# Top-k masks, the order of the search, and the order of weight halves in a hybrid attention block

## The chip, the cores and the metric

The kernel runs on one core of a Trainium2 chip. A core has a matrix engine (TensorE, PE), three engines for elementwise work (VectorE or DVE, ScalarE or ACT, GpSimd or POOL), a queue that issues transfers (SyncE or SP) and 16 DMA engines. Each engine takes its instructions in a fixed order and waits on semaphores for the others. The metric is the device time of one execution in microseconds (us).

## The reference

One decoder block on x of 1024 tokens by 1024 channels, in float32. Two branches read the same projection `h @ w_in`: RWKV-7 time mixing, and sparse attention in which an indexer picks 256 keys for each query. The two are gated, projected and added to x; a squared-ReLU MLP follows. What matters here is the selection:

```python
logits = jnp.einsum('bqhd,bsd->bqhs', qi_b, ki)
score = jnp.einsum('bqh,bqhs->bqs', wi_b, jax.nn.relu(logits)).astype(f32)
causal = key_pos[None, :] <= qpos[:, None]
score = jnp.where(causal[None], score, -jnp.inf)
_, idx = lax.top_k(score, topk)                 # topk = 256
...
s = jnp.einsum('bqhd,bqkd->bqhk', q_b, k_sel) * (ATT_HEAD_DIM ** -0.5)
s = jnp.where(valid[:, :, None, :], s, -jnp.inf)
p = jax.nn.softmax(s, axis=-1)
```

Of equal scores at the threshold, `top_k` takes those with the lowest index.

## The kernel before

Work goes through in phases: norm and transposition of x; the projections of the attention branch; indexer scores; the search for each query's 256th largest score; masks; attention; the RWKV recurrence; gates and output projection; the MLP. Matrix products keep float32 accuracy by splitting both operands into a high and a low part and adding three products (`mm3`, L242 to L245, and `mm3y`, L195 on, which goes through `mm`, L190). A weight tile is loaded (`st`), its high part is taken by ScalarE (L210) and its low part by GpSimd, or by VectorE where that is asked for (L211). Split weights live in a ring of three buffers (`w`).

*Projections by tokens* (`in_a`, L293 on). For the keys and values, the indexer queries and the attention queries, 256 columns at a time. The weights come as two tiles, `ws[0]` for the input channels 0 to 511 and `ws[1]` for 512 to 1023. For each half of the tokens and each pair of 128-token tiles, one accumulation buffer (`dn`, two of them) takes tile j = 0 through all eight channel blocks k, then tile j = 1. ScalarE evicts it (L306), and rotary embedding follows on GpSimd (L381) and VectorE (L382 to L386).

*Gate projections* (`gates`, L444 on). A generator of 16 units of eight steps for one half of the tokens, 24 matmuls to a unit, then an eviction by ScalarE (L453) and a transfer out (L454). It fills PE while the scores are made; what is left runs after the last query projection.

*Selection* (`select`, L538 on). Query blocks 0 and 1 have no more than 256 keys and need no search. The six others are searched by two generators: `([3, 4, 5], True)` counts with ScalarE, `([2, 6, 7], False)` with VectorE. A score is turned into a sortable 32-bit key, whose high and low 16 bits are searched one after the other, 16 bisection steps each. ScalarE counts by summing signs (L593) with the bookkeeping on GpSimd (L595 to L603); VectorE counts with a comparison that accumulates (L578) and does its own bookkeeping (L583, L584). Between the two searches the low keys are clipped against the high result (L614 to L616, on VectorE for both generators). After the second, the threshold is put together from both results (L621 to L626) and the mask of each block is made on VectorE (L634 to L641): 0 for a chosen key, -BIG for another, written over the scores `sc[b]`.

*Order.* The two generators are advanced in turns (loop at L825). In turns 19 and later, the list `SPREAD` says how many steps of the RWKV projections (`rwkv_in`, eight steps to a half of one unit, 24 matmuls and an eviction) are pulled after the turn. `RIN[0]`, 114, is the number of those steps ahead of attention; `RIN[0] - QF - early` of them, with `early` what the turns have taken, come after the masks, then the load and split of the first queries (`q_split`), then `QF` = 8 more. The eviction of such a half is ScalarE's at L673 and VectorE's at L674 (and, for the column between halves, L679 and L681). A planner lays out each engine's queue from this program order with a simulated time; `in_order` and `after` add order without a wait: an operation passed to `in_order` stands in VectorE's queue behind the one last stored in `own["V"]`. During the searches the first count of each step and each eviction at L674 are chained in this way.

*Buffers.* The mask's three work tiles (`ge`, `eq`, `cs`), the keys, ScalarE's junk output and attention's scores and split queries share one ring of six buffers (`t4`). Attention (`att_s`, L765 on) adds `sc[b]` to the raw scores and takes the maximum in one operation (L782).

## Time and profile before

| | |
|---|---|
| median of 3 runs | 1784.76 us (1780.63 to 1793.0) |
| the profiled execution | 1787.29 us |
| its span, first to last instruction | 1785.5 us |
| PE busy over the span | 1685.5 us (94%) |
| VectorE busy over the span | 1336.4 us (75%) |
| mean granted clock of PE | 0.972 |

The durations below are of the one profiled execution. In a row of the profile, "L593 ACT ACTIVATE jk<-room,neg" is line 593, ScalarE, an activation that writes the tile `jk` from `room` and `neg`. A group gives count, busy time and mean; a wait gives who waited, for whom, the total in us, how often, and the longest. "PEld" is the loading of weights into PE, beside the matmuls. A row of the order of time starts with start and duration in us, and may end with the idle time before it and what ended it.

### The profile page before, as it was taken

How to read it: one execution, taken by the hardware profiler on the slowest of the kernel's cores; microseconds unless marked ns; L12 is line 12 of the kernel's file. 1: busy time of each engine (PE TensorE's matmuls, PEld its weight loads, DVE VectorE, ACT ScalarE, POOL GpSimd, SP SyncE). 2: the span in 40 equal slices, each digit the busy share in tenths (PEclk: the TensorE clock that was granted, in tenths of full speed). 3: DMA queues.
4: the chain of work that ended last, by engine and by line, in shares of the span. 5: the costliest groups of instructions: out<-in, count | busy, mean ns of one | idle time of the engine just before them, and what ended most of it. 6: DMA issues, size and time to landing. Idle time of an engine off the chain costs nothing.

```text
span 1785.5 us, 27137 instructions
## 1 busy us (share of the span) xinstructions
PE 1685.5 (94%) x9554; PEld 1415.8 (79%) x9554; DVE 1336.4 (75%) x2610; ACT 894.3 (50%) x1751; POOL 821.8 (46%) x749
## 2 busy tenths in 40 slices
PE   6999899889999989998999998999999999999997
PEld 6988887778888777786777887877888888888885
DVE  6689989986777374767665546799988875865988
ACT  5376667547777434354535425553444444444443
POOL 1522564334443243344424532486766655545552
PEclk9999999999999998999887999999999999999999
DMA  5230254223211455355345567416444358643544
GB/s 176 78 118 27 81 154 118 73 69 112 100 30 52 138 148 139 91 146 164 102 116 166 172 196 282 124 54 212 154 157 168 130 185 307 204 147 101 146 144 142
DMA packets 268287, 242.04 MB, mean 136 GB/s; under 512 B 64284, under 2 KB 206934, under 8 KB 268150
## 3 DMA queue, kind: packets, MB, share of 16 engines
q1 hardware_dynamic: 268150, 240.30, 43.1%
q8 instruction: 75, 1.23, 0.3%
q14 instruction: 62, 0.51, 0.1%
HBM read 164.76 MB, written 75.50 MB: 135 GB/s over the span
## 4 chain that ended last, share of the span: by engine, by line
PE 56%; DVE 21%; DMA 7%; ACT 5%; issue 5%; POOL 4%; SPq 1%; POOLq 0%; DVEq 0%; ACTq 0%
PE up L190 24%; PE dn L190 11%; PE sm L190 9%; DVE jk L578 2%; PE sm L193 2%; PE ch L190 2%; DVE w L1348 2%; DMA zt<-zd 2%; PE acc L190 2%; PE dn L245 1%; PE dn L244 1%; PE dn L243 1%; ACT jk L593 1%; DVE LT L958 1%; DVE Z L1020 1%
## 5 line engine op out<-in xcount | busy, mean ns | idle before, releaser
L190 PE MATMUL dn<-hT,w 128*128 128x512 f32 (+1 forms) x1488 | 380.0, 403 | 11.4 <-ACT ev L453 4.5
L190 PEld LDWEIGHTS dn<-hT,w 128*128 128x128 f32 (+1 forms) x1488 | 274.1, 189 | 72.0 <-ACT ev L453 5.3
L190 PE MATMUL up<-h,w 128*128 128x512 f32 x1344 | 310.4, 391 | 6.1 <-DVE w L1348 3.3
L190 PEld LDWEIGHTS up<-h,w 128*128 128x128 f32 x1344 | 251.1, 188 | 62.4 <-DVE w L1348 5.0
L1348 DVE TENSOR_TENSOR w<-st,w 128x512 fp32r<-128x512 f32 x216 | 215.5, 1031 | 75.6 <-ACT w L1347 75.5
L211 POOL TENSOR_TENSOR w<-st,w 128x1024 fp32r<-128x1024 f32 (+2 forms) x75 | 183.3, 2445 | 186.8 <-ACT w L210 153.1
L190 PE MATMUL up<-w 128*128 128x512 f32 x1008 | 246.1, 390 | 3.6 <-DVE w L1348 3.5
L190 PEld LDWEIGHTS up<-w 128*128 128x128 f32 x1008 | 188.7, 188 | 45.4 <-DVE w L1348 6.4
L1347 ACT ACTIVATE w<-st 128x512 fp32r<-128x512 f32 x216 | 128.1, 625 | 159.2 <-PE up L190 50.9
L1641 POOL TENSOR_TENSOR st<-wb,wb 128x512 f32<-128x512 f32 x80 | 120.0, 1503 | 94.5 <-DVE w L1348 74.3
L1503 POOL TENSOR_TENSOR c<-st 128x512 f32<-128x512 f32 x80 | 125.4, 1576 | 50.2 <-DMA st<-in_w_ffn_up 23.7
L210 ACT ACTIVATE w<-st 128x1024 fp32r<-128x1024 f32 (+2 forms) x91 | 94.6, 1041 | 46.6 <-PE acc L245 15.4
L1514 POOL TENSOR_TENSOR C<-C 128x512 f32<-128x512 f32 x64 | 75.9, 1186 | 56.5 <-ACT C L1513 56.5
L578 DVE TENSOR_SCALAR_CACHE_REDUCE jk<-room,cand 128x384 bf16<-128x384 int16 (+2 forms) x96 | 97.1, 1012 | 2.9
L593 ACT ACTIVATE jk<-room,neg 128x512 bf16<-128x512 int16 (+2 forms) x96 | 78.5, 819 | 34.4 <-POOL neg L601 26.7
L243 PE MATMUL dn<-w,hT 128*128 128x256 f32 (+1 forms) x320 | 92.4, 291 | 3.5 <-ACT w L210 2.6
L244 PE MATMUL dn<-w,hT 128*128 128x256 f32 (+1 forms) x320 | 92.1, 289 | 3.5 <-DVE w L211 3.5
L788 POOL TENSOR_SCALAR sm<-sm,rs 128x128 f32<-128x128 f32 (+7 forms) x64 | 47.7, 747 | 102.5 <-DVE rs L787 58.6
L245 PE MATMUL dn<-w,hT 128*128 128x256 f32 (+1 forms) x320 | 91.8, 289 | 0.0
L1348 DVE TENSOR_TENSOR w<-c,w 128x512 fp32r<-128x512 f32 x80 | 82.9, 1048 | 0.4 <-ACT w L1347 0.3
L190 PE MATMUL sm<-w 128*128 128x512 f32 x288 | 81.0, 389 | 0.0
L1347 ACT ACTIVATE w<-c 128x512 fp32r<-128x512 f32 x80 | 48.8, 626 | 58.3 <-PE up L190 46.0
(332 smaller groups left out, 3519.9 us busy)
## 6 DMA issues: line engine op xcount, KB each, us to landing
st<-hcd SPq DMA_DIRECT2D x112, 256.0 KB
st<-in_w_in SPq DMA_DIRECT2D x54, 512.0 KB
st<-in_w_ffn_up SPq DMA_DIRECT2D x36, 512.0 KB
hcd<-C SPq DMA_DIRECT2D x16, 1024.0 KB
wb<-in_w_ffn_down SPq DMA_DIRECT2D x64, 256.0 KB
hcd<-kc SPq DMA_DIRECT2D x16, 768.0 KB
zd<-ev SPq DMA_DIRECT2D x20, 512.0 KB
gzd<-ev SPq DMA_DIRECT2D x32, 256.0 KB
```

The costliest lines, as they stand in the source:

```text
L190: pe(nc.tensor.matmul(*args, **kw))
L210: nc.scalar.activation(hi, st[0:rows, 0:n], AF.Copy)
L211: (eng or nc.gpsimd).tensor_tensor(lo, st[0:rows, 0:n], hi.bitcast(F32), op=OP.subtract)
L243: nc.tensor.matmul(ps, l[0], r[0], start=start, stop=False, skip_group_check=shared)
L244: nc.tensor.matmul(ps, l[0], r[1], start=False, stop=False, skip_group_check=shared)
L245: nc.tensor.matmul(ps, l[1], r[0], start=False, stop=stop, skip_group_check=shared)
L578: ins = nc.vector.tensor_scalar(jk[:, 0:(b + 1) * P], src[b], cand[:, j:j + 1], None, op0=OP.is_ge, op1=OP.add, accum_out=cnt[:, j:j + 1])
L593: nc.scalar.activation(junk, src[b], AF.Sign, bias=neg[:, j:j + 1], accum_out=cnt[:, j:j + 1])
L1347: nc.scalar.activation(hi, src, AF.Copy)
L1348: return eng.tensor_tensor(lo, src, hi.bitcast(F32), op=OP.subtract)
L1503: nc.gpsimd.tensor_tensor(c, src, blocks[LEFT[p][2]], op=OP.add if LEFT[p][1] == "+" else OP.subtract)
L1641: nc.gpsimd.tensor_tensor(c, src, wblocks[RIGHT[p][2], f], op=OP.add if RIGHT[p][1] == "+" else OP.subtract)
```

## The change

Five things are edited.

- `select`, masks: the comparison that counts is now "not above the threshold" and its result `ge` is kept; equality is written as 0 or BIG, so that its running sum counts in BIG; the number of equal keys still wanted comes from the count alone, `(count + 256 - n) * BIG`; and the last operation puts `ge * -BIG` and the chosen equal keys together. BIG becomes a power of two. Six operations over a block's columns become five.
- `select`, order: ScalarE's generator yields three more turns before its thresholds and masks, and each generator yields after each mask but its last. A mask's first operation is in order behind `own["V"]`, its last is stored there. So VectorE's own blocks 2, 6, 7 come first, then 3, 4, 5.
- `SPREAD` has five entries more, 8 steps each, so that an RWKV half with its eviction is pulled behind each of the first five masks; 40 steps fewer come after the masks.
- `gates` keeps its evictions in a list, and the first Sign of ScalarE's low search is put behind the third last of the 16 of `gates(1, ...)` in ScalarE's queue.
- `in_a`: the weight half `kh` becomes the outermost loop inside an accumulation buffer: both tiles take channel blocks 0 to 3, then both take 4 to 7.

```diff
--- before.py
+++ after.py
@@ -32,9 +32,9 @@
 FF = 4096
 DEC = float(np.exp(-0.5))
 NEG = -3.0e38
-BIG = 1.0e30
+BIG = float(2 ** 100)
 PE_WINDOW = 32
-SPREAD = [0, 0, 0, 0, 0, 8, 8, 8, 8, 0, 8, 8, 8, 0, 8]
+SPREAD = [0, 0, 0, 0, 0, 8, 8, 8, 8, 0, 8, 8, 8, 0, 8, 8, 8, 8, 8, 8]
 FILL = [8, 2, 40, 3, 6, 22]
 AHEAD = [6, 6, 6, 0, 0, 0, 0, 0, 1, 1, 0, 10]
 FIN_LAG = 5
@@ -297,12 +297,11 @@
             z = ev4()
             for pr in range(2):
                 ps = dense()
-                for j in range(2):
+                for kh, j, k in [(kh, j, 4 * kh + i) for kh in range(2) for j in range(2) for i in range(4)]:
                     t = 2 * pr + j
-                    for k in range(8):
-                        mm3(ps[:, j * 256:j * 256 + n], [hT[half][k][:, s_, t * P:(t + 1) * P] for s_ in range(2)],
-                            [ws[k // 4][:, s_, k % 4, :] for s_ in range(2)],
-                            start=(k == 0 and j == 0), stop=(k == 7), shared=True)
+                    mm3(ps[:, j * 256:j * 256 + n], [hT[half][k][:, s_, t * P:(t + 1) * P] for s_ in range(2)],
+                        [ws[kh][:, s_, k % 4, :] for s_ in range(2)],
+                        start=(k == 0 and j == 0), stop=(k == 7), shared=True)
                 nc.scalar.activation(z[:, pr * 512:(pr + 1) * 512].rearrange("p (t c) -> p t c", t=2)[:, :, 0:n],
                                      ps.rearrange("p (t c) -> p t c", t=2)[:, :, 0:n], AF.Copy)
             evac(half, z)
@@ -441,6 +440,8 @@
         return [(w_in[:, C_GATE + u * P:C_GATE + (u + 1) * P].rearrange("(k p) n -> p k n", p=P), [8, P])
                 for u in range(16)]
 
+    gate_ev = []
+
     def gates(hf, mul, ws):
         for u in range(16):
             w = next(ws)
@@ -450,7 +451,7 @@
                     mul(ps, w[:, a_, k, :], hT[hf][k][:, b_, :], start=(k == 0 and i == 0), stop=(k == 7 and i == 2))
                 if k == 7:
                     e = ev4()
-                    nc.scalar.activation(e[:, 0:512], ps, AF.Copy)
+                    gate_ev.append(nc.scalar.activation(e[:, 0:512], ps, AF.Copy))
                     nc.sync.dma_start(gz_dram[u // 8, u % 8, :, hf * 512:(hf + 1) * 512], e[:, 0:512])
                 yield
 
@@ -590,7 +591,10 @@
             for k in range(15, -1, -1):
                 for j, b in enumerate(blocks):
                     junk = t4b("jk", (b + 1) * P, BF16)
-                    nc.scalar.activation(junk, src[b], AF.Sign, bias=neg[:, j:j + 1], accum_out=cnt[:, j:j + 1])
+                    ins = nc.scalar.activation(junk, src[b], AF.Sign, bias=neg[:, j:j + 1],
+                                               accum_out=cnt[:, j:j + 1])
+                    if src is lo and k == 15 and j == 0:
+                        after(gate_ev[-3], ins)
                 up, _ = step_of(k)
                 nc.gpsimd.tensor_tensor(ok, cnt, need, op=OP.add)
                 nc.gpsimd.tensor_scalar(ok, ok, 1.0, -1.0, op0=OP.min, op1=OP.max)
@@ -618,9 +622,11 @@
             yield
         yield from search(lo)
         thr, ti = sm_("thr"), sm_("ti", I32)
+        for _ in range(3 if act else 0):
+            yield
         in_order(nc.vector.tensor_copy(ti, th))
         nc.vector.tensor_scalar(ti, ti, 16, None, op0=OP.logical_shift_left)
-        nc.vector.tensor_scalar(tl, cand, 32768.0, None, op0=OP.add)
+        in_order(nc.vector.tensor_scalar(tl, cand, 32768.0, None, op0=OP.add))
         nc.vector.tensor_tensor(ti, ti, tl, op=OP.bitwise_or)
         nc.vector.tensor_scalar(tl, ti, 31, 0x7FFFFFFF, op0=OP.arith_shift_right, op1=OP.bitwise_and)
         nc.vector.tensor_tensor(thr.bitcast(I32), ti, tl, op=OP.bitwise_xor)
@@ -631,14 +637,16 @@
             ge = t4("ge")[:, 0:n]
             eq = t4("eq")[:, 0:n]
             cs = t4("cs")[:, 0:n]
-            nc.vector.tensor_scalar(ge, sc[b], t_ap, None, op0=OP.is_ge, op1=OP.add, accum_out=cnt[:, j:j + 1])
-            nc.vector.tensor_scalar(eq, sc[b], t_ap, None, op0=OP.is_equal)
+
+            in_order(nc.vector.tensor_scalar(ge, sc[b], t_ap, None, op0=OP.is_le, op1=OP.add,
+                                             accum_out=cnt[:, j:j + 1]))
+            nc.vector.tensor_scalar(eq, sc[b], t_ap, BIG, op0=OP.is_equal, op1=OP.mult)
             nc.vector.tensor_tensor_scan(cs, eq, eq, 0.0, op0=OP.add, op1=OP.max)
-            nc.vector.scalar_tensor_tensor(gen[:, j:j + 1], cs[:, n - 1:n], float(TOPK), cnt[:, j:j + 1],
-                                           op0=OP.add, op1=OP.subtract)
+            nc.vector.tensor_scalar(gen[:, j:j + 1], cnt[:, j:j + 1], float(TOPK - n), BIG, op0=OP.add, op1=OP.mult)
             nc.vector.scalar_tensor_tensor(cs, cs, gen[:, j:j + 1], eq, op0=OP.is_le, op1=OP.mult)
-            nc.vector.scalar_tensor_tensor(cs, sc[b], t_ap, cs, op0=OP.is_gt, op1=OP.add)
-            nc.vector.tensor_scalar(sc[b], cs, BIG, -BIG, op0=OP.mult, op1=OP.add)
+            own["V"] = nc.vector.scalar_tensor_tensor(sc[b], ge, -BIG, cs, op0=OP.mult, op1=OP.add)
+            if j + 1 < m_:
+                yield
 
     own = {}
 
```

## The prediction

> **What bounds the kernel now.** I read the page's head first, then busy time by stage, then the waits of VectorE and of TensorE (PE) inside the stages that the change touches, then VectorE's groups and order in the mask stage.
>
> ```profile
> span 1785.5 us, 27137 instructions
> PE 1685.5 (94%) x9554; PEld 1415.8 (79%) x9554; DVE 1336.4 (75%) x2610; ACT 894.3 (50%) x1751; POOL 821.8 (46%) x749
> ```
>
> Over the whole span PE is the bound, at 94%. But the change lies inside the first 385 us, so I cut that part by stage, in the view of windows. Columns: window, length, then busy time (and instructions) of PE, weight loads, DVE, ACT, POOL, then granted clock, DMA share, GB/s.
>
> ```profile
> 171.00:272.00 101.00, 95.75 (x537) 84.62 (x537) 93.87 (x189) 60.29 (x125) 57.73 (x94) 0.97 0.41 118
> 272.00:342.40 70.40, 63.60 (x269) 50.80 (x267) 66.63 (x141) 54.88 (x120) 31.61 (x73) 0.98 0.30 90
> 342.40:384.40 42.00, 35.97 (x150) 28.19 (x150) 41.93 (x70) 8.18 (x14) 13.79 (x6) 0.96 0.25 79
> 384.40:420.00 35.60, 34.87 (x195) 29.43 (x196) 21.02 (x93) 25.42 (x70) 16.42 (x21) 1.00 0.27 75
> ```
>
> These are, roughly, the search through the high halves of the keys, the search through the low halves, the masks, and the start of attention. In the mask stage VectorE is busy 41.93 of 42.00 us, and PE only 35.97. PE then has its filler work (projection steps, handed out in a fixed number before attention) finished and stands until VectorE comes free. In both search stages VectorE is also nearly full, 93.87 of 101 and 66.63 of 70.4. From 384.4 on it is half idle and PE is the bound again. So the time at which attention starts is set by VectorE, in one line of work from about 171 to 384 us: keys, 16 steps, remainders, 16 steps, masks. Where does that line itself stand still? The view of waits, VectorE, 155 to 385 us:
>
> ```profile
> DVE q L614 <- POOL neg L589: 3.8, 1, 3.8
> DVE ev L674 <- ACT ev L673: 1.2, 1, 1.2
> DVE rm L382 <- ACT ev L306: 0.9, 1, 0.9
> ```
>
> Together 5.9 us. PE's own waits are larger; the first three rows are 160 to 300 us, the next three the mask stage:
>
> ```profile
> PE dn L190 <- ACT ev L453: 4.5, 2, 4.1
> PE dn L244 <- DVE w L211: 3.5, 2, 2.2
> PE dn L243 <- ACT w L210: 2.6, 1, 2.6
> ...
> PE dn L190 <- DVE ev L674: 3.7, 2, 2.4
> PE acc L190 <- DVE mx L782: 2.0, 1, 2.0
> PE dn L190 <- DVE ti L621: 1.8, 1, 1.8
> ```
>
> 10.6 and 7.5 us. The change aims at nearly all of these 18.1 us. My choice, on which everything hangs: a PE stall ahead of 384 us is worth only what it takes off VectorE's line, because the steps that PE may run before attention are a fixed number (114) and it is through with them before VectorE is.
>
> **The masks, five wide operations instead of six.** VectorE's groups in the mask stage, 342.4 to 384.4 us (count, busy us, mean ns):
>
> ```profile
> L636 DVE TENSOR_TENSOR_SCAN cs<-eq 128x512 f32<-128x512 f32 (+5 forms) x6 | 9.7, 1615 | 0.0
> L640 DVE SCALAR_TENSOR_TENSOR cs<-sc,thr,cs 128x512 f32<-128x512 f32 (+5 forms) x6 | 7.7, 1285 | 0.0
> L639 DVE SCALAR_TENSOR_TENSOR cs<-cs,gen,eq 128x512 f32<-128x512 f32 (+5 forms) x6 | 6.5, 1087 | 0.0
> L634 DVE TENSOR_SCALAR_CACHE_REDUCE ge<-sc,thr 128x512 f32<-128x512 f32 (+5 forms) x6 | 5.6, 926 | 0.0
> L674 DVE SCALAR_TENSOR_TENSOR ev<-dn,par,ev 128x511 f32<-128x511 f32 x7 | 5.2, 738 | 0.0
> L635 DVE TENSOR_SCALAR eq<-sc,thr 128x512 f32<-128x512 f32 (+5 forms) x6 | 3.5, 579 | 0.0
> L641 DVE TENSOR_SCALAR sc<-cs 128x512 f32<-128x512 f32 (+5 forms) x6 | 3.1, 516 | 0.0
> L637 DVE SCALAR_TENSOR_TENSOR gen<-cs,cnt 128x1 f32<-128x1 f32 x6 | 2.0, 329 | 0.0
> L625 DVE TENSOR_SCALAR tl<-ti 128x3 int32<-128x3 int32 x2 | 0.2, 166 | 0.0
> ```
>
> What goes is L641, 3.1 us. L635 gains a multiply by BIG in the same pass; L641 already does two operations in one pass and is no slower for it, so 0. L637 stays a one-column operation, 0. The last step reads `ge` where L640 read the scores: same form, 0.
>
> **Masks and evictions in strict turn.** Before, the planner mixes the operations of several masks. After, each mask begins behind an eviction, and the eviction stands behind the mask's last operation, so a mask's own chain runs by itself. What that costs is seen in VectorE's order of time (start, duration):
>
> ```profile
> 344.14 0.48 DVE L635 TENSOR_SCALAR eq<-sc,thr 128x512 f32<-128x512 f32 x1
> 344.65 1.23 DVE L636 TENSOR_TENSOR_SCAN cs<-eq 128x512 f32<-128x512 f32 x1
> ...
> 346.58 0.55 DVE L635 TENSOR_SCALAR eq<-sc,thr 128x640 f32<-128x640 f32 x1
> 347.04 0.74 DVE L674 SCALAR_TENSOR_TENSOR ev<-dn,par,ev 128x511 f32<-128x511 f32 x1
> ```
>
> The scan reads what L635 writes and starts 0.03 us after its end; the eviction, which needs nothing of L635, starts 0.09 before its end. An unmixed mask has three such boundaries (L635 to the scan, then to each of the last two): 3 x 6 x 0.12 = 2.2 us at most, 0 if the planner finds something to put between; most of the boundaries before were mixed, so I take 1.9. For the same reason the removed L641 is worth 3.1 less six overlaps of 0.07 to 0.09, 2.6. And the thresholds, computed before for both searches in alternation (five operations of about 0.16 us, of which L625 is one), now stand apart, three turns later for ScalarE's blocks: five more at 0.16 and the gap of 0.03, +1.0. The mask stage by itself therefore comes to -2.6 + 1.9 + 1.0 = +0.3 us: nothing. The 7.5 us of PE waits there change their place, not their sum:
>
> ```profile
> 335.14 5.74 PE L190 MATMUL dn<-hT,w 128*128 128x512 f32 x24 [0.33 <-ACT last L679]
> ```
>
> A projection half takes PE 5.74 us, two halves fit into the `dn` buffers, and a mask of mean width (704 columns: 1.6 + 2 x 1.1 + 0.9 + 0.6 = 5.3 us by the groups' means) with its eviction of 0.7 takes VectorE longer.
>
> [...]
>
> **ScalarE's search behind due evictions.** ScalarE's order of time, and the split on GpSimd (POOL) ahead of it:
>
> ```profile
> 256.93 4.31 POOL L211 TENSOR_TENSOR w<-st,w 128x1024 fp32r<-128x1024 f32 x1 [3.17 <-ACT w L210]
> ...
> 271.21 0.72 ACT L593 ACTIVATE jk<-room,neg 128x512 bf16<-128x512 int16 x1 [7.52 <-DVE room L616]
> ...
> 276.42 0.58 ACT L453 ACTIVATE ev<-dn 128x512 f32<-128x512 f32 x1
> ```
>
> The queue stands 7.52 us at the first Sign of the low search, and the thirteenth gate eviction stands behind it; PE waits 4.1 for that. After, the thirteenth and fourteenth come first. PE gets the 4.1 back. ScalarE's low search starts two or three us later, which costs nothing: its thresholds are wanted three turns and three masks later than before. PE then waits at the in-order evictions of the search instead. What VectorE gains is its 1.2 us at L674, a half that came late. -1.2.
>
> **Weight halves outermost.** The first half of a projection's weights serves 24 matmuls before the second is needed, not 12, and is free 24 matmuls before the end. ScalarE at the second query projection:
>
> ```profile
> 182.57 1.04 ACT L210 ACTIVATE w<-st 128x1024 fp32r<-128x1024 f32 x1
> ...
> 196.73 0.60 ACT L306 ACTIVATE ev<-dn 128x512 f32<-128x512 f32 x1 [4.28 <-PE dn L245]
> ```
>
> The earlier release lets L210 go ahead of a round of three Signs (the shortest, above, takes 0.72), and the 1.3 us of the other L211 wait is covered by the 12 more matmuls. PE's eviction at 196.73 comes earlier, ScalarE's high search, which stood 4.28 behind it, ends earlier, and with it the threshold on which VectorE waits 3.8 at L614. That chain has the split at 256.93 in it, which can keep the wait: bounds 0 and -3.8, and I take -2.5. The 0.9 at L382 goes too. Both bounds of the ends: if nothing moves, 0 of 3.4.
>
> **Sum.** +0.3 - 1.2 - 2.5 - 0.9 = -4.3 us on the profiled run's 1787.29 (span 1785.5 and 1.8 around it): 1783.0. The median of the three runs, 1784.76, is 2.5 below the profiled run; on that scale 1780.5, and I say 1780.
>
> **The rivals.**
>
> *PE's stalls count in full.* If evictions let VectorE, too, run on sooner, PE's 18.1 us come out, and the clock lost after them: 0.03 x 101 + 0.02 x 70.4 + 0.04 x 42 = 6.1. Half to all of 24.2: 1761 to 1773. For it: PE is at 94% and the chip's bound later. Against: VectorE's 41.93 of 42.00.
>
> *Nothing moves.* The split at 256.93 keeps L614's wait, the mask stage is at +0.3: 1784 to 1786. The planner, which orders queues by a simulated time, may also cover what the trace shows open.
>
> *Attention starts late (slower).* The score tiles come from a ring of six buffers (`t4`), three to a mask, and `ge` now lives to the end of its mask. The queries of block 0 take the first buffer of the last mask but one; before, that was free early (its mask was long past L634). The chain behind it:
>
> ```profile
> 370.07 0.62 ACT L422 ACTIVATE hl<-qz 128x512 fp32r<-128x512 f32 x1
> 370.77 1.81 POOL L423 TENSOR_TENSOR hl<-qz,hl 128x512 fp32r<-128x512 f32 x1 [1.20 <-ACT hl L422]
> 376.29 1.03 PE L431 MATMUL sm<-cst,hl 128*128 128x128 f32 x8
> 378.92 1.08 ACT L433 ACTIVATE qs<-sm 128x512 fp32r<-128x512 f32 x2
> ...
> 353.01 2.82 DVE L640 SCALAR_TENSOR_TENSOR cs<-sc,thr,cs 128x512 f32<-128x512 f32 x1
> ...
> L211 POOL TENSOR_TENSOR w<-st,w 128x1024 fp32r<-128x1024 f32 x3 | 10.9, 3648 | 28.2 <-ACT w L210 28.2
> ```
>
> 0.6 + 1.8 + 1.0 + 1.1 and some 0.8 of handing over are 5.3 us, against a last mask of 768 columns (5.3 x 768 / 704 = 5.8) and an eviction of 0.7. It decides when L423 has to queue behind a weight split of 3.6 us: then the chain is 8.9 against 6.5, attention starts 2.4 later, and PE, through with its steps, stands. With the searches' gains absent, and one more collision like L640's 2.82 (0.74 in L674's similar form, so 2.1 lost), +0.3 + 2.4 + 2.1 = +4.8: 1790. [...]
>
> **Chances.** VectorE's line, -4.3 (from -8, no ordering cost and the whole wait gone, to -1): 0.55. PE's stalls: 0.13. Nothing: 0.17. Late attention: 0.15. The range takes in the first and third whole and most of the others: 1768 to 1792. Faster or slower by over 1% (17.8 us; about what one measurement can tell, the runs before spread over 12.4): faster, the better half of the second, 0.08; slower, the fourth with a re-planned order elsewhere on top, 0.03; within, 0.89.
>
> **What would show it.** Right: VectorE still busy over 97% in the mask stage, which lasts 41 to 43 us; L641's group gone; L453 no longer behind the first Sign; a wait of VectorE at the threshold under 2 us; attention beginning at 379 to 382. PE idle ahead of attention still over 10 us. Wrong: a mask stage of under 37 us with PE idle under 3, or first attention scores waiting on L422 or L423 with VectorE idle.

## The result, and the profile after

The changed kernel takes 1815.59 us (median of 6 runs, 1806.5 to 1819.6) beside 1785.24 (median of 6) of the kernel before: ratio 1.0143, 95% interval 1.0110 to 1.0175. Run twice more, the ratio was 1.0108 (1.0075 to 1.0142) and 1.0087 (1.0057 to 1.0116). Over its 18 runs the mean is 1810.4, and over 112 runs of the kernel before 1789.4: it is 21.1 us slower (standard error 1.2), not 4.3 faster. Four single runs of 2058 to 2351 us, at mean clocks of 0.65 to 0.75, are left out of every mean here.

The head of the page of the changed kernel, then four stages in the view of windows (columns as in the prediction; the last is the recurrence from its first to its thirteenth chunk, which no edit touches). Between lines 300 and 440 the changed kernel's line numbers are one lower than before's, from 640 on eight higher.

```profile
span 1817.8 us, 27139 instructions
PE 1706.6 (94%) x9554; PEld 1433.3 (79%) x9554; DVE 1340.8 (74%) x2604; ACT 894.2 (49%) x1751; POOL 814.2 (45%) x749
```

```profile
276.00:349.00 73.00, 60.55 (x253) 48.62 (x251) 67.74 (x141) 52.70 (x118) 29.40 (x72) 0.93 0.25 73
349.00:392.10 43.10, 35.65 (x145) 28.23 (x146) 42.39 (x64) 8.30 (x14) 10.75 (x6) 0.92 0.23 71
392.10:409.60 17.50, 17.20 (x84) 14.22 (x84) 7.88 (x41) 10.36 (x30) 5.69 (x8) 0.90 0.12 45
704.40:1000.30 295.90, 266.80 (x1850) 221.77 (x1850) 187.17 (x567) 121.97 (x265) 99.94 (x98) 0.82 0.42 118
```

The last two of these stages in the kernel before:

```profile
694.50:968.90 274.40, 250.48 (x1842) 207.83 (x1842) 187.02 (x566) 122.25 (x264) 102.03 (x98) 0.87 0.45 126
384.30:399.30 15.00, 14.35 (x78) 12.01 (x78) 7.84 (x42) 10.18 (x29) 5.71 (x8) 1.00 0.17 38
```

The low search begins at 276.0, not 272.0 (+4.0), and lasts 73.0, not 70.4 (+2.6); the masks last 43.1, not 42.0 (+1.1); attention's first block 17.5, not 15.0 (+2.5), at a granted clock of 0.90 where it was 1.00. That is 10.2 us by the second block (10.5 between the means of three profiles of the one and two of the other). From there to the first chunk the distance stays (+9.9). The recurrence then takes 21.5 more, at a clock of 0.82 against 0.87. Two different losses, then.

**The first loss.** VectorE's order of time in the changed kernel (the last remainders of its own blocks, the first of ScalarE's, then two evictions of the column between halves), and GpSimd's weight splits in the same kernel:

```profile
263.22 5.89 DVE L620 TENSOR_SCALAR room<-q 128x384 int16<-128x384 f32 x3
269.04 3.61 DVE L618 TENSOR_SCALAR q<-room,th 128x512 f32<-128x512 int16 x3
...
331.84 2.37 DVE L689 SCALAR_TENSOR_TENSOR ev<-last,par,ev 128x1 f32<-128x1 f32 x1
...
343.28 2.45 DVE L689 SCALAR_TENSOR_TENSOR ev<-last,par,ev 128x1 f32<-128x1 f32 x1
```

```profile
262.21 5.81 POOL L211 TENSOR_TENSOR w<-st,w 128x1024 fp32r<-128x1024 f32 x2
269.57 2.66 POOL L211 TENSOR_TENSOR w<-st,w 128x1024 fp32r<-128x1024 f32 x1 [1.55 <-ACT w L210]
...
331.79 2.40 POOL L211 TENSOR_TENSOR w<-st,w 128x1024 fp32r<-128x1024 f32 x1 [0.47 <-ACT w L210]
343.31 2.40 POOL L211 TENSOR_TENSOR w<-st,w 128x1024 fp32r<-128x1024 f32 x1 [0.47 <-ACT w L210]
```

L620's operations and an eviction of the column in the kernel before:

```profile
257.49 1.49 DVE L616 TENSOR_SCALAR room<-q 128x384 int16<-128x384 f32 x3
...
328.38 0.21 DVE L681 SCALAR_TENSOR_TENSOR ev<-last,par,ev 128x1 f32<-128x1 f32 x1
```

An operation on one column takes 0.21 us, and 2.37 when a split of 2.40 runs beside it: it lasts as long as the split. Before, one of the search's four took that long (2.38), after two (2.37 and 2.45).

**What became of the waits.** First VectorE's waits from 155 to 392 us, all there are; then TensorE's largest; then ScalarE, VectorE and TensorE in order of time at the largest of those:

```profile
DVE ev L682 <- ACT ev L681: 2.7, 3, 1.2
DVE sc L509 <- ACT rl L505: 2.1, 5, 0.9
```

```profile
PE dn L190 <- ACT last L687: 12.8, 4, 9.8
PE dn L244 <- DVE w L211: 3.9, 1, 3.9
PE sm L430 <- POOL hl L422: 2.9, 1, 2.9
```

```profile
304.59 0.17 ACT L687 ACTIVATE last<-dn 128x1 f32<-128x1 f32 x1 [7.83 <-DVE ev L682]
...
303.81 0.75 DVE L682 SCALAR_TENSOR_TENSOR ev<-dn,par,ev 128x511 f32<-128x511 f32 x1
...
304.81 7.57 PE L190 MATMUL dn<-hT,w 128*128 128x512 f32 x21 [9.76 <-ACT last L687]
```

The threshold wait of 3.8 and PE's 4.1 behind the first Sign are gone. But PE's first RWKV half, now done earlier, is still evicted by VectorE only behind its step of turn 24, at 303.81; ScalarE's copy of the last column is in ScalarE's queue behind that, with the whole search behind the copy, and PE stands 9.76 for both: more than all it had won.

**The second loss** is the clock. TensorE stands 3.64 us in the first inversion of the recurrence, and the product that follows runs at half speed (3.62 us for all 16 of its matmuls; 1.97 in a run below, at a clock of 1.00). TensorE's order of time there, changed kernel, and the next 35 us in windows of 5:

```profile
709.05 3.20 PE L190 MATMUL sm<-P,bd 128*128 128x32 f32 x14 [3.64 <-ACT bd L1073]
```

```profile
709.40:714.40 5.00, 5.00 (x27) 4.68 (x26) 1.90 (x6) 1.64 (x6) 0.00 (x0) 0.50 0.31 102
714.40:719.40 5.00, 5.00 (x17) 3.64 (x17) 1.60 (x2) 2.81 (x8) 1.60 (x3) 0.50 0.02 6
719.40:724.40 5.00, 5.00 (x25) 4.01 (x24) 4.42 (x17) 0.00 (x0) 0.25 (x2) 0.50 0.25 79
724.40:729.40 5.00, 5.00 (x29) 3.99 (x29) 3.96 (x9) 3.39 (x9) 1.98 (x4) 0.50 0.25 80
729.40:734.40 5.00, 5.00 (x20) 4.18 (x19) 2.67 (x10) 1.24 (x3) 0.26 (x1) 0.59 0.31 105
734.40:739.40 5.00, 4.88 (x60) 4.11 (x59) 4.83 (x18) 1.68 (x6) 1.56 (x4) 1.00 0.18 55
```

The column before the last two is the granted clock: 0.50 for some 27 us, with TensorE shown busy all the time. In the kernel before the same stand is 2.63 and is followed by 10 us of it:

```profile
698.42 3.62 PE L190 MATMUL sm<-P,bd 128*128 128x32 f32 x16 [2.63 <-ACT bd L1065]
```

Theory 1 is that the 21.5 us more come from the queues of this stage, which the planner laid out anew; Theory 2, from the later start; Theory 3, formed on the way, that they are the granted clock, which differs between executions. Theories A and B are on the front: VectorE's own line, or ScalarE's and PE's stands.

### The profile page after: what moved, and what is told of

Its sections match the earlier page's. It is cut to its first block, busy times and chain, and to the rows that moved or that the text cites. A ratio compares the mean times of both kernels' runs of the same rounds, so it can differ in the third digit from the quotient of the medians.

```text
span 1817.8 us, 27139 instructions
## 1 busy us (share of the span) xinstructions
PE 1706.6 (94%) x9554; PEld 1433.3 (79%) x9554; DVE 1340.8 (74%) x2604; ACT 894.2 (49%) x1751; POOL 814.2 (45%) x749
## 4 chain that ended last, share of the span: by engine, by line
PE 54%; DVE 20%; DMA 6%; issue 4%; ACT 4%; POOL 2%; SPq 0%; DVEq 0%; POOLq 0%; ACTq 0%
PE up L190 25%; PE dn L190 12%; PE sm L190 8%; DVE jk L579 4%; PE sm L193 2%; DVE w L1356 2%; PE ch L190 2%; PE acc L190 2%; DMA zt<-zd 2%; POOL w L211 1%; PE acc L244 1%; PE acc L243 1%; PE acc L245 1%; DVE x L1709 1%; DMA st<-ytd 1%
## 5 line engine op out<-in xcount | busy, mean ns | idle before, releaser
L190 PE MATMUL dn<-hT,w 128*128 128x512 f32 (+1 forms) x1488 | 384.5, 407 | 17.8 <-ACT last L687 12.8
L190 PEld LDWEIGHTS dn<-hT,w 128*128 128x128 f32 (+1 forms) x1488 | 278.2, 191 | 79.2 <-ACT last L687 14.5
L211 POOL TENSOR_TENSOR w<-st,w 128x1024 fp32r<-128x1024 f32 (+2 forms) x75 | 179.4, 2393 | 195.4 <-ACT w L210 178.4
```

Of the source, the lines that this page charges most:

```text
L190: pe(nc.tensor.matmul(*args, **kw))
L211: (eng or nc.gpsimd).tensor_tensor(lo, st[0:rows, 0:n], hi.bitcast(F32), op=OP.subtract)
```

## The experiments

The measure for the recurrence is its length and its granted clock from first to thirteenth chunk in the profile; the product of the two is my estimate of its length at full clock (16 matmuls of 32 columns take 3.62 us at a clock of 0.50 and 1.94 at 1.00; the rounding of the clock alone makes it uncertain by 1.4). "Mean" is the mean of all runs less that of before (1789.4; standard errors 1 to 2). "Less front" takes off what attention's second block comes later than 399.5, so it is what is lost or won behind the front; the front is that of one profile, and profiles start some 2 us apart. "Places" are queue places of the recurrence planned otherwise than in before, of some 1630; 348 is the changed kernel's own set.

| kernel | mean | mean clock | second block at | less front | recurrence | its clock | product | places |
|---|---|---|---|---|---|---|---|---|
| before, two profiles | 0 | 0.968 | 399.3, 399.8 | 0 | 274.4, 274.3 | 0.87, 0.88 | 239, 241 | 0 |
| five operations | +1.5 | 0.965 | 401.0 | 0 | 276.4 | 0.88 | 243 | 0 |
| weight halves | -3.0 | 0.970 | 402.2 | -5.7 | 271.5 | 0.88 | 239 | 101 |
| halves and five | +5.5 | 0.965 | 402.1 | +2.9 | 281.6 | 0.84 | 237 | 101 |
| all but gate order | +3.3 | 0.966 | 402.4 | +0.4 | 268.8 | 0.89 | 239 | 145 |
| delay before masks | +10.6 | 0.965 | 408.0 | +2.1 | 289.3 | 0.83 | 240 | 34 |
| all, other queues | +12.5 | 0.965 | 409.7 | +2.3 | 279.3 | 0.87 | 243 | 33 |
| all, first half earlier | +14.3 | 0.965 | 407.6 | +6.2 | 285.8 | 0.84 | 240 | 130 |
| gate order, four memsets | +14.0 | 0.963 | 405.8 | +7.7 | 283.7 | 0.83 | 235 | 216 |
| all, two halves earlier | +17.1 | 0.965 | 408.5 | +8.1 | 284.5 | 0.86 | 245 | 348 |
| gate order only | +18.5 | 0.959 | 409.4 | +8.6 | 288.5 | 0.84 | 242 | 348 |
| changed, three profiles | +21.1 | 0.962 | 409.6, 409.4, 411.1 | +10.6 | 295.9, 282.8, 283.5 | 0.82, 0.87, 0.86 | 243, 246, 244 | 348 |

Of kernels that change one thing or nothing, many runs lie over 20 us apart (before: 1778 to 1805), and the clock tells them apart: over the 112 runs of before, 0.01 more of mean clock goes with 13.1 us less (correlation -0.92; 2.6 us of scatter stay around the line). "At equal clock" below means along this line.

**Each part alone.** The first Sign of the low search behind the gate eviction, in an otherwise unchanged kernel:

```diff
+                    if src is lo and k == 15 and j == 0:
+                        after(gate_ev[-3], ins)
```

> The kernel before with one edit alone: the first Sign of ScalarE's low search stands behind the third last gate eviction. Nothing in the recurrence is edited, yet the planner then gives the recurrence the same queues, row by row, as in the changed kernel. Theory 1 (the recurrence's queues were planned anew, and worse): from the first to the thirteenth chunk 290 to 300 us (274 before, 296 after), attention starts within 3 us of before, total +15 to +25. Theory 2 (the recurrence is slower because it starts later and on a colder clock after the masks): 272 to 278 us, total -3 to +4.

1807.14 us, ratio 1.0106 (1.0076 to 1.0136): this edit alone makes nearly all the difference, 18.5 of 21.1 us in the mean. Attention starts at 391.6, 7.4 later than before, where within 3 had been expected; its second block comes at 409.4 as in the changed kernel; but 2.2 of these 10 us lie ahead of ScalarE's first eviction (31.9, before 29.7), where nothing is edited. ScalarE stands 7.9 us at the copy of the last column, as there. The long recurrence (288.5) I put down to the queues then, which here are those of the changed kernel, row for row; a single profile doesn't carry that, as the next runs show.

The masks in five operations (the five lines of the diff in the mask, and `BIG`), nothing else:

> The kernel before with the masks in five wide operations alone; no order is edited, and the recurrence has the queues of before. Both theories: recurrence 272 to 278 us. The mask stage is shorter by the removed operation, 2 to 3 us, if VectorE bounds it; total -4 to 0.

Ratio 1.0012 (0.9981 to 1.0044); the mean, +1.5, is above the -4 to 0 expected. From first mask to attention 40.1 us, not 40.8, where 2 to 3 less were expected. VectorE was through earlier, but then it stood at the first maximum, for PE:

```profile
385.23 0.29 DVE L780 CUSTOM_DVE_ANT_0 sm<-acc,sc 128x128 f32<-128x128 f32 x1 [2.63 <-PE acc L190]
```

So PE's lead at attention is small: with VectorE's line 3 us shorter, PE sets the start.

The weight half outermost in `in_a`, nothing else:

> The kernel before with the weight halves outermost alone. The key-value projection at 40 to 60 us loses 2 to 3 us as in the changed kernel (the last of its evictions at 52.3 against 49.6), and attention starts 0 to 3 us later. Theory 1: the recurrence has other queues again (about one row in sixteen differs from before), so anything from 270 to 285 us. Theory 2: 272 to 278 us. Total 0 to +12 against 0 to +5.

Ratio 0.998 (0.9951 to 1.0009): nothing that can be measured, and a mean 3.0 below before, where 0 to 12 above were expected. VectorE stands 4.6 us less between its first count and the low search, and L616 takes 4.4 us more there, beside a split that now falls on it.

Both of these, without the two edits of order:

> Weight halves outermost and five operations to a mask, without the two edits of order. The recurrence's queues are those of weight halves alone. As the sum of the two alone: attention's start at 385.5 to 388.5 (+2.9 and +1.0 at most, masks 0.7 shorter), the recurrence 270 to 274, the end at 1780 to 1785; a ratio of 0.996 to 1.000 to the kernel before. If the two edits of order are what makes the changed kernel slower, this one is not slower; if the halves or the masks cost it, it is above 1.003.

Ratio 1.0035 (0.9999 to 1.0071), 5.5 above before and not faster; at equal clock +1.2. Its queues in the recurrence are those of the halves alone, place for place, and yet the recurrence took 10 us longer. The two rows, halves alone first:

```profile
694.50:966.00 271.50, 249.64 (x1849) 206.79 (x1849) 188.71 (x561) 121.80 (x265) 102.30 (x99) 0.88 0.46 128
```

```profile
697.60:979.20 281.60, 261.72 (x1848) 215.53 (x1847) 189.47 (x561) 122.16 (x266) 103.24 (x99) 0.84 0.44 123
```

Same queues, other clock, other length: the queues alone don't set the length of one execution. The ratio over 1.003, which I had named as the sign of a cost of these edits, is clock too: at equal clock 1.2 (error 0.9) is left.

All edits but the gate order:

> All edits but one: the first Sign of ScalarE's low search is not put behind the third last gate eviction. The planned queues of the recurrence are a third set here: some 145 of 1630 places away from those of before, 378 away from those of the changed kernel. Theory 1 (the loss in the recurrence comes with the particular queues that the gate order brought): first to thirteenth chunk in 270 to 282 us as in the kernels near to before (274.4; 276.4; 271.5; 279.3), not 288 to 296; the end at 1778 to 1795 us. Rival (the order of masks and halves lengthens it): 288 or more, the end above 1800. Up front: if the gate order alone costs the time before attention, the first maximum of attention comes at 385 to 388 (before 384.3, weight halves alone 387.2, five operations alone 385.2); if the order of masks and evictions costs it too, at 390 or later.

Ratio 1.0024 (0.9992 to 1.0055); attention starts at 387.3. The recurrence (268.8) was even under the 270 to 282 forecast, the other two held. Without the one edit the changed kernel loses nothing that can be measured in its runs, though its front is 3 us later.

**What each edit costs up front.** Counted from the end of ScalarE's first eviction (29.7 to 31.9 us), which no edit touches, the stages begin at:

| kernel | VectorE's first low count | first mask | first maximum | second block |
|---|---|---|---|---|
| before, two profiles | 242.2, 240.5 | 313.8, 312.2 | 354.6, 353.0 | 369.6, 369.5 |
| weight halves | 243.3 | 314.9 | 356.3 | 371.3 |
| all but gate order | 243.7 | 315.6 | 357.5 | 372.6 |
| gate order only, and with four memsets (below) | 243.8, 242.3 | 318.8, 317.1 | 359.7, 358.1 | 377.5, 375.9 |
| changed, three profiles | 245.5, 246.4, 246.1 | 319.6, 320.0, 320.4 | 361.7, 362.1, 362.5 | 379.1, 378.9, 380.0 |

In the means, all edits put 8.3 us on the first maximum, the gate order alone 5.1, the others together 3.7. Half of the gate order's part lies in the low search: from VectorE's first low count to the end of its last it takes 71.6 to 72.3 us in the five profiles with that edit, 69.5 to 69.9 in the other four. The other half is a weight split that the earlier gate eviction lets through, the one at 269.57 above. It falls on the remainders of ScalarE's blocks, whose first three operations took 3.61 us there; with the halves alone no split runs beside them:

```profile
269.42 1.47 DVE L613 TENSOR_SCALAR q<-room,th 128x512 f32<-128x512 int16 x3
```

**The same edits, other queues.** `gate_ev[-2]` in place of `gate_ev[-3]`, and the gate order alone with four clearings ahead of the recurrence:

```diff
-                        after(gate_ev[-3], ins)
+                        after(gate_ev[-2], ins)
```

> The changed kernel with one index altered: the Sign stands behind the second last gate eviction instead of the third last. All five edits are in it, and selection and masks go the same way; but the recurrence now has nearly the queues of before (33 of 1630 rows differ). Theory 1: recurrence 272 to 282 us, attention starts at about 392 as in the changed kernel, total +6 to +14. Theory 2: recurrence 290 to 300 us and total +25 to +33, as in the changed kernel.

```diff
         nc.gpsimd.memset(sbd[i], 0.0)
+    for i in range(4):
+        nc.gpsimd.memset(sbd[i % 2], 0.0)
```

> The gate order alone (e_gate_only: 1807.1 median) plus four clearings of a 128 x 512 tile on GpSimd right before the recurrence, which add work and are useless in themselves; everything ahead of it stays as in e_gate_only (attention's start 391.6, the first chunk at 704), but the planner lays the recurrence's queues out anew: 216 of 1630 places from those of before, 440 from those of e_gate_only. Theory 1 (these queues cost the time): first to thirteenth chunk in 270 to 283 us in place of 288.5, the end 5 to 18 us earlier than 1808.9, though work was added. Theory 2 (it is slower because it starts later): 288 or more and the end at 1808 to 1812.

Ratios 1.0073 (1.0046 to 1.0101) and 1.0074 (1.0043 to 1.0105). By their recurrences (279.3; 283.7, just over the 283) both spoke for Theory 1. The means say how far it goes: the first has the changed kernel's front and, behind it, before's queues but for 33 places, and is 8.6 us faster than the changed kernel. The second gains 4.5 on the gate order alone, of which 3.6 are its earlier front, and 1.9 of these lie ahead of the first eviction.

**Is it ScalarE's stand?** The first two RWKV halves of the low search pulled earlier, then only the first:

```diff
-SPREAD = [0, 0, 0, 0, 0, 8, 8, 8, 8, 0, 8, 8, 8, 0, 8, 8, 8, 8, 8, 8]
+SPREAD = [0, 0, 0, 8, 0, 8, 0, 8, 8, 0, 8, 8, 8, 0, 8, 8, 8, 8, 8, 8]
```

> The changed kernel with the first two RWKV halves of the low search pulled after turns 22 and 24 in place of 24 and 25; the queues of the recurrence are planned as in the changed kernel, row for row. In the changed kernel ScalarE stands some 8 us at its copy of the last column (L687), behind VectorE's eviction that has its place after turn 24, and PE stands 9.8 behind that. Theory A (attention starts when VectorE's own line ends, and that was stretched by GpSimd's weight splits beside its operations, not by ScalarE's stand): the stand at L687 falls under 3 us, ScalarE's last Sign comes 4 to 9 us earlier than 344.6, and attention starts where it did, 390 to 394. Theory B (the stand of ScalarE and PE delays attention): it starts at 383 to 387. Recurrence, first to thirteenth chunk: 288 to 297 by Theory 1, since its queues are those of the changed kernel; the end at 1805 to 1818.

```diff
+SPREAD = [0, 0, 0, 8, 0, 0, 8, 8, 8, 0, 8, 8, 8, 0, 8, 8, 8, 8, 8, 8]
```

> The changed kernel with only the first RWKV half of the low search pulled three turns' places earlier (after turn 22, not 24; the second as before). The recurrence's queues are planned in another way than in the changed kernel (408 of 1630 places), 130 from those of before. Front: ScalarE's stand at the last column falls from 9 us to under 3; attention's second block starts 1 to 3 us earlier than in the changed kernel (407 to 409; with both halves earlier it was 408.5 at a beginning that was 1.2 later). Theory 3: length of the recurrence times clock 236 to 244 and the mean of the runs 1 to 4 us below or above the 1804.7 of both halves earlier, as the clock comes out. Theory 1: the queues are near to those of before, so the recurrence takes 270 to 280 and the runs are 10 to 17 us below 1804.7.

Ratios 1.0105 (1.0074 to 1.0135) and 1.0084 (1.0051 to 1.0116). The stand of 7.8 at the copy did not go: it split into three and two (6.7 and 5.4 in all, the longest 4.7), so that forecast was wrong; PE's wait behind it fell from 12.8 to 7.0 and 3.9. ScalarE's last Sign came 2.0 and 0.8 earlier than 344.6, not 4 to 9. Attention started at 391.5 and 391.1 all the same: Theory A. ScalarE's and PE's stands are not what delays it. (For the recurrence Theory 1 had the first at 288 to 297 and the second at 270 to 280; they took 284.5 and 285.8.)

**A pure delay.** Five useless counts in VectorE's line ahead of the first mask, in the kernel before:

```diff
+        for _ in range(0 if act else 5):
+            own["V"] = in_order(nc.vector.tensor_scalar(jk, lo[blocks[-1]], cand[:, 0:1], None, op0=OP.is_ge,
+                                                        op1=OP.add, accum_out=ok[:, 0:1]))
         in_order(nc.vector.tensor_copy(ti, th))
```

> The kernel before with five useless counts over 1024 columns (1.36 us each, 6.8 together) in VectorE's line right ahead of the first mask; the recurrence's queues are those of before but for 34 of some 1630 places. If VectorE's line sets the start of attention, attention starts 6.8 later, at 390 to 392, although PE has no more to do. Theory 3 (an up-front delay passes through whole, and what lies above it in the changed kernel is the granted clock of the recurrence, which differs between executions of one kernel): the mean of the runs is 6 to 9 us above that of before, and the recurrence, length from first to thirteenth chunk times granted clock, stays at 236 to 244. Theory 2 (a later start makes the recurrence itself slower): 15 us or more above before.

Ratio 1.0065 (1.0036 to 1.0094), 10.6 above before (standard error 2.0; Theory 3 had 6 to 9); attention at 390.9 (+6.6), its second block at 408.0 (+8.8). So the delay passes through whole, and 2.2 are added in attention's first block:

```profile
390.90:408.00 17.10, 16.47 (x78) 13.71 (x78) 10.00 (x43) 9.86 (x29) 6.79 (x8) 0.86 0.09 20
```

PE, with its steps done, stands longer, and the clock is 0.86 over that block, 1.00 before (0.90 in before's second profile, where the block took 16.6). Behind the block 2.1 are left, with an error as large: a later start by itself costs the recurrence little or nothing (Theory 2 falls), although this profile's recurrence took 289.3.

**The same kernels again.**

> The changed kernel itself, a second time, for a second profile and twelve more runs. Its first profile had 295.9 us from first to thirteenth chunk at a granted clock of 0.82; before had 274.4 at 0.87. Theory 3 (the clock that was granted is most of the difference, and it is in part chance): the clock of the recurrence is another, 0.82 to 0.87, the length goes with it so that length times clock stays at 240 to 245, and the end of the profiled run is anywhere from 1800 to 1820; the mean clock of all runs is near 0.961 again if it belongs to the kernel, and nearer to 0.968 (before) if it was chance. Theory 1 (the new queues alone): 293 us or more at whatever clock. Up front the same as in the first profile within 3 us: attention's second block at 407 to 412.

> The changed kernel a third time. Its mean over twelve runs is 1811.8 at a mean clock of 0.9618. Again 1808 to 1815 and 0.960 to 0.964. In the profile, attention's second block at 407 to 412 (before 399 to 400), first chunk to the last output projection 362 to 390 us, of which 326 to 336 would be left with the time at half clock taken as half: the length is another one each time, the rest is not. If instead the queues set the length, it stays at 375 to 388 with the same stretches in the same places.

> The kernel before, for a second profile of it. Theory 3: with the same queues the recurrence takes 270 to 290 us from first to thirteenth chunk, as the clock comes out (0.89 to 0.83), and length times clock is 236 to 243 again; up front attention starts at 384 to 388. Theory 1 (queues alone set the length): 273 to 276 at whatever clock. The ratio to the kernel before is 1 within its interval.

The changed kernel's recurrence, second and third profile, each from its own trace, then before's second:

```profile
705.00:987.80 282.80, 250.16 (x1837) 207.95 (x1837) 186.40 (x567) 122.18 (x265) 100.56 (x98) 0.87 0.44 122
```

```profile
706.40:989.90 283.50, 252.74 (x1839) 210.16 (x1839) 187.92 (x567) 122.02 (x265) 100.42 (x98) 0.86 0.43 122
```

```profile
695.10:969.40 274.30, 251.16 (x1845) 207.34 (x1845) 187.08 (x567) 122.48 (x265) 102.14 (x98) 0.88 0.45 126
```

One program, 295.9, 282.8 and 283.5: the first profile had 13 us more, at a lower clock, and the end moved with it (spans 1817.8, 1807.2, 1806.5); the front did not. Means of 1808.8 and 1807.7 follow 1814.8. Before again: ratio 0.9993 (0.9955 to 1.0031), and its recurrence, 274.3, fits both theories. But what I had given as the sign of Theory 1 in the third run came as well: 375.4 us from the first chunk to the last output projection, 334.4 with half clock counted half, and the second and third profile have the same first stretches of half clock in the same places (24 us at the first chunk, then 10, 7, 3, 3 and 3), as before's two have theirs (10 there, later 14 and 20). So the queues set where TensorE stands and the clock falls; how long it stays down differs between executions (27, 24 and 24 us at the first chunk in the three of the changed kernel). Over many runs this shows in "less front": the three kernels with the changed kernel's queues lose 8.1 to 10.6 behind the front, those within 34 places of before 0 to 2.3. Counted from the first eviction it is 10.0 to 11.3 against 0.2 to 3.2. The products of the changed kernel (243 to 246) are some 4 above before's two, but the five operations, on before's queues, have 243 too; the rest is half clock. Nor is the loss bound to this one set of queues: the sets 130 and 216 places from before lose 6.2 and 7.7, the one 145 places away 0.4. Against it stand the halves, -5.7 alone and +2.9 with five operations on the same queues: that much two kernels can differ for a reason not found here.

**Does the stand set off the half clock?** Four useless matmuls where TensorE stands in the first inversion, in before, in the changed kernel and with the weight halves:

```diff
         pv = four_heads(R32)
+        if g == 0:
+            warm = small()
+            for i in range(4):
+                ins = nc.tensor.matmul(warm, cst[:, 0:128], cst[:, 0:512], start=True, stop=True)
+                after(pe_hist[-1], ins)
+                pe_hist.append(ins)
```

> The kernel before with four useless matmuls (128x512, full float32, on constants; they add work and change no value) in the place where TensorE stands 2.6 us between the two four-head products of the first inversion. Theory 3a (the stand sets off the half-clock stretch that follows): the stretch of 10 us at the first chunk is gone, first to second chunk falls from 38.1 to 32 to 36 us, the mean granted clock of the runs rises by 0.002 to 0.005, and the mean falls 2 to 8 us below before (ratio 0.995 to 0.999). Theory 3b (the small matmuls around it leave TensorE too little active): the stretch stays, 10 to 34 us as before, and the mean is 0 to 3 us above before.

> The changed kernel with the same four matmuls. Its recurrence's queues are planned nearer to before (119 of 1630 places) than to the changed kernel (293). Theory 3a: the stretch of 23 to 27 us at the first chunk is gone, first to second chunk falls from 44 or 45 to 32 to 36 us, the mean is 6 to 14 us below the changed kernel's 1811.8 (12 runs). Theory 3b: it stays and the mean is 1808 to 1815. Attention's second block at 407 to 412 in both.

> Weight halves alone with the same four matmuls: the version that would be best if both help. Theory 3a: mean 3 to 9 us below before, ratio 0.995 to 0.998. Theory 3b: no better than weight halves alone (0.998, interval 0.995 to 1.001).

TensorE's order of time in the changed kernel with the stand filled, and windows over the next 15 us:

```profile
702.89 3.68 PE L1074 MATMUL sm<-cst 128*128 128x512 f32 x8
706.41 0.39 PE L190 MATMUL ch<-sbd,X 128*128 128x128 f32 x2
706.63 1.97 PE L190 MATMUL sm<-P,bd 128*128 128x32 f32 x16
```

```profile
707.50:712.50 5.00, 5.00 (x37) 4.05 (x37) 2.29 (x7) 3.17 (x9) 0.72 (x3) 1.00 0.34 108
712.50:717.50 5.00, 5.00 (x41) 4.15 (x42) 4.65 (x14) 2.32 (x5) 1.82 (x4) 1.00 0.01 2
717.50:722.50 5.00, 4.52 (x31) 3.37 (x30) 4.07 (x16) 2.41 (x8) 0.68 (x1) 1.00 0.49 157
```

The 27 us of half clock are gone, the product over P takes 1.97 where it took 3.62, and first to second chunk 37.6 us (32 to 36 expected), not 45.0. In all three kernels the stretch that began at this stand is gone with it (before has 3.4 us of half clock at 708.5, behind another stand of 1.2 us), and in all fifteen profiles that have the stand it is there: without the stand, no stretch (Theory 3a). The changed kernel falls to a mean of 1797.1, 13.3 below itself, ratio 1.0029 (1.0004 to 1.0055) to before; what is left, 7.7 us, is no more than its delay up front (second block at 408.3). Part of the gain can be its queues, now 119 places from those of before. But before and the halves came out at 1.0022 (0.9998 to 1.0046) and 1.0029 (0.9999 to 1.0059), 6.0 and 6.7 above before: where I had expected a gain. The halves with the stand filled have even a slightly higher mean clock than alone (0.971, 0.970), so their loss is not clock alone. Each has 27 us of half clock some 90 us later instead, where before had none; the planner had laid the queues out anew for each (in before 341 places). One stand filled moves the others, and none of these versions beats the kernel before.

## Why the prediction was wrong

**The marks, and which engine sets the start of attention: right in the main.** The mask stage of 41 to 43 us (43.1), L641's group gone, the gate eviction ahead of the first Sign, the threshold wait under 2 us came as named, the last for another reason than mine (below); attention at 379 to 382 did not (392.1). PE's idle time of over 10 us did not come in the mask stage either: it was 7.45 there, and 6.03 before. VectorE is busy 42.39 of 43.10 us (98%) in that stage, and 6.8 us put into its line came out as 6.6. But the choice on which all hung, PE through before VectorE, holds only within some 3 us: with the five operations alone VectorE had to wait for PE.

**Masks, +0.3: measured +1.1.** L641's group is gone, and alone the five operations gave -0.7 from first mask to attention. In the changed kernel three one-column evictions take 4.8 us in that stage, two of them (2.33 and 2.25) beside splits again:

```profile
L689 DVE SCALAR_TENSOR_TENSOR ev<-last,par,ev 128x1 f32<-128x1 f32 x3 | 4.8, 1594 | 0.0
```

So the size of the term is about right, in part by luck: not only the order makes it.

**ScalarE's search behind due evictions, -1.2: the step that failed first.** I wrote that the later search "costs nothing" and that PE "gets the 4.1 back", and counted L674's wait as gained. PE did get it back, and that did no good: its half then had to wait for VectorE's place in the turn, and gave back 9.76. The eviction that came earlier was followed by an earlier split of the next weights, and that fell on VectorE's operations. Instead of -1.2 the edit put 5.1 us on the start of attention by itself: some 2 in the remainders, and some 2.5 in the low search, of which 2.2 are the second L689 of 2.4 us. In the gate order alone the split hit the next three operations instead (L615's kind, 4.48 us, not 2.28). I had moved evictions past queues and followed ScalarE's and PE's, not GpSimd's, although I had used just such a collision in a rival for a mask (L640's 2.82 us, beside a split of 3.50 at 351.78).

**Weight halves, -2.5 and -0.9: the waits went, but not by my mechanism, and nothing was gained.** I had ScalarE's eviction at 196.73 come earlier, its high search end earlier, and with it the threshold. Counted from the first eviction, over all profiles:

| | seven profiles without the edit | eleven with it |
|---|---|---|
| that eviction (the 17th of L306) begins | 165.4 to 167.5 | 169.2 to 169.5 |
| GpSimd has the threshold ready | 230.9 to 234.3 | 231.6 to 234.8 |
| VectorE's first high count | 140.8 to 141.5 | 147.6 to 148.0 |
| its last high count | 219.5 to 222.9 | 224.2 to 225.3 |
| its own remainders end | 227.2 to 230.5 | 234.2 to 239.5 |

The eviction came later and the threshold no earlier. The waits at L614 and L382 are not among VectorE's waits after because VectorE itself comes later: that the mark was met is luck. In the halves alone the 4.6 us of waits were filled by 4.4 more in L616 (in the changed kernel L620's 5.89 us against 1.49). I had given the split at 256.93 as the reason for the bound of 0, and taken -2.5. Why VectorE's first count comes over 6 us later is not settled. It is not the first projection, whose fourth eviction comes some 2 us later in nine of the eleven profiles: in the other two it does not, and the first count is as late.

**What the sum left out: the clock.** I counted a PE stand ahead of attention as costless because PE has no more to do. But the stand (386.7 to 389.6) is followed by time at half clock (0.50 from 388.7 to 395.6), and most of that falls into attention's first block, where PE is the bound again: +2.5, and +2.2 with the pure delay. Not all of that is the change's: before's second profile has 16.6 us and a clock of 0.90 there too, so that between the means of the profiles the difference is 1.5. With the 2.5 of the first profiles, 4.0 + 2.6 + 1.1 + 2.5 = 10.2 us up front.

**The rest of the 21: the re-planned order.** I had it "elsewhere on top" of a rival, with 0.03, and the sum had nothing for it. The planner places by simulated time, and a first Sign put behind an eviction at 270 us gave the recurrence another order from 690 us on. The three kernels with that order lose 8 to 11 us there: 2 to 4 in length at full clock, the rest in half clock (likely, by three kernels, and not shown beyond the scatter that the halves' two rows have; two other orders lose 6 and 8). What makes an order slow stays open. The mean clock of the changed kernel's 18 runs is 0.0059 below before's, worth 7.8 us along the line; 13.3 (error 1.0) remain at equal clock: the 10.2 up front, a part of which is clock itself, and at least 3 more. The changed kernel's first profile alone, with 21.5, would have said twice as much.

**The rivals.** PE's stands in full, and nothing moving: no. Late attention, the slower one, gave the right sign by the wrong chain. Its wait is there (PE at L430 for `hl`, 2.9; before's L431 and L423), but it is there as well with all edits but the gate order, where attention starts at 387.3, and VectorE is busy up to 0.13 us before the first maximum: the late queries can cost no more than that. The result lies outside all four cases, since none had a loss up front and one behind it.

**The range.** It rested on one profiled run. The kernel before has 27 us between its own executions, most of it with the clock, and the changed kernel 13 between two profiles of a stage that the change does not touch; a shift up front can't be read from the end of one run.

## What to carry to other kernels

An earlier release moves whatever it releases: follow the freed buffer to the next load and the next split, and look which operation then runs beside that split (here 0.21 us became 2.37). Where an in-order queue holds a step at a fixed place in a turn, freeing its input earlier only lengthens the wait for that place, and all that is queued behind it (7.83 us here, and 9.76 on the engine behind). Where a planner lays out the queues, a change early on re-orders stages that nobody edited (348 of some 1630 places here): compare their means over kernels with the same and with other queues, multiply a length by its granted clock, and profile the same kernel twice before one trace is believed (295.9 us at 0.82 and 282.8 at 0.87 were one program).

## What the hardware showed

- Around TensorE's stand in the first inversion (2.50 and 2.63 us in before's two profiles, 2.59 to 3.91 in others) the clock fell to 0.50, for 10 us in before's two and for 14 to 34 in the others, with TensorE shown busy from the end of the stand on. A longer stand did not mean a longer stretch: 34 us went with 2.59, 14 with 3.91. In windows of 1 us the stretches of half clock in the recurrence came to 3.4, 7, 10, 14, 17, 20, 24, 27, 31 or 34 us: steps of 3.4. A product of 16 matmuls of 32 columns takes 3.62 in such a stretch, 1.94 outside.
- Stands of 2.5 and 2.6 us were enough. In eight of the fifteen profiles with the stand the clock is recorded at 0.50 within 1 us of TensorE's stop (0.77 after it in the changed kernel's first), and half speed lasts for up to ten of these steps (34 us) although the trace shows TensorE busy. Why stays open; the matmuls before and behind the stand are small (64x64, and 32 columns).
- In this kernel the clock is no small matter: in 112 runs of one program the mean clock went from 0.957 to 0.976, and the time from 1805 to 1778.
